# Plain fp32 matmuls in the w_o and S5 projections, DMAs taken off GpSimd's queue, and a larger weight pool, in a two-block fp32 model on one core

## The chip, the core and the metric

The kernel runs on one core of a Trainium2 chip, as one launch. The engines are TensorE (PE: matmul and transposes; its weight loads show as PEld), VectorE (DVE), ScalarE (ACT), GpSimd (POOL) and SyncE (SP), which here only issues DMAs. Each runs its own instructions in order and waits on semaphores. The metric is device time in microseconds from start to end of one execution; smaller is better.

## The reference

The input x has 256 tokens of 1024 features, all in fp32. The first block is attention and a mixture of experts, the second an S5 mixer, a gated FFN with a causal convolution (ffn0), a forgetting attention (fox) and another FFN (ffn1), and a last norm.

```python
h = rms_norm(x, ln1_g); z = h @ w_in                       # first block
o_a = window_gqa(q_a, k_a, v_a, rel_bias, a_sink)          # 8 heads of 64, window 128
o_b = latent_attention(c_q, c_kv, k_rope, ...)             # 8 heads, 64 + 32 rotated
x = x + concat([rms_norm(o_a), rms_norm(o_b)]) @ w_o       # 1024 x 1024
x = x + expert_choice_ffn(rms_norm(x), w_router, w_gate, w_up, w_down)   # 16 experts of 1024 x 1024 x 3
# second block; shift, scale, gate = silu(c) @ ada_w + b, four times
u = h @ w_in; hs = scan(lb, u @ bb); y = gelu(hs @ c + d * u)            # S5, complex diagonal state
m = (y * sigmoid(y @ w_glu)) @ w_out
h = h + gate * m;  h = h + gate * conv_ffn(...)            # 1024 -> 2 x 2816 -> 1024
F = cumsum(log_sigmoid(h @ w_f + b_f)); s = q.k / 8 + F[t] - F[s]        # fox, causal, 16 heads
h = h + gate * (softmax(s) @ v @ w_out);  h = h + gate * conv_ffn(...)
```

## The kernel before

The stages run one after the other: attention, experts, S5, ffn0, fox, ffn1, final norm. Activations sit on the 128 partitions, either by token (two halves of 128) or by feature (8 x 128).

**Matmuls.** Most large projections use `mm3` (line 367): both operands are split into a rounded part and a rest (`hi`, `lo`, type fp32r), and three matmuls are added up, hi x hi, hi x lo and lo x hi. `mm` (line 360) issues one matmul; on plain fp32 operands it shows as two records in the trace. The experts' gate and up projections and the attention scores are already plain. A `Pair` holds hi and lo; `split` (line 397) makes one from a result in PSUM, hi by ACT and lo by DVE.

**Weights.** `plan` (line 225) lists loads in the order in which they are to be issued. `fill` (line 259) issues them on SP's queue, each into a slot of 8 KB per partition (1 MB in all), as long as slots are free:

```python
while self.pos < min(n, len(self.loads)) and self.used + self.room + max(0, self.hires - self.his) < NSLOT and self.wused < self.cap:
```

`prep` (line 271) splits a weight that has landed: `whi` on ACT (for w_oa and w_ob on POOL, line 287) and `wlo` on DVE or on POOL (line 291), into two further slots, and the raw one is freed. `done` gives slots back when the last matmul has been issued, and calls `fill` again. NSLOT is 22. `MIDS` (9) is the number of 2 KB tiles that `m2k` hands out in turn (`z`, `rot`, `g`, `sq` and others). `weights(room, look, hires)` sets per stage how many slots are kept back. Room for both and for GpSimd's DMA ring comes from the same memory.

**Attention** (`attn_block`). Scores, softmax and weighting run by head pairs; `finish` (line 960) scales an output and splits it into `o`; `w_o` (line 1024) multiplies by w_oa or w_ob, 4 x 4 x 2 matmuls of 512 columns, each as three. `bqk`, `p`, `mx` and `bkT` are tiles of the latent heads' queries and keys, the softmax and the transposed keys. While this runs, `fill` fetches the first experts' w_gate and w_up.

**S5** (`s5`, line 1465). `u(n)` (n = 0 to 3) is a projection of 256 features, followed by a transpose into `V` on DVE. `states(n)` multiplies by a table `S`, copies PSUM to `z` on ACT, transposes to `re` and `im`, turns them by cos and sin on DVE and POOL (tiles `rot`), scans along the chunk on DVE, and turns back. `outputs(n)` makes `y`, gelu on ACT, transposes it on DVE (`yt`) and splits it (`yh`, `yl`). `glu(n)` multiplies by w_glu, 64 matmuls of 256 columns in all, each as three. The order written in the code is u0, u1, states 0, u2, states 1, outputs 0, u3, states 2, outputs 1, states 3, outputs 2 and 3, then glu and the output projection (`acc`); a scheduler orders each engine's instructions from it.

**Fox** (`fox`, line 1740). The forget gate's cumulated logs `F` are written to DRAM (`f_dram`) and read back as `nF`, broadcast over partitions, both on POOL's queue. `project_v` and `project` use twelve slices of fox_w_in. Rows of gates go through DRAM as well (`row_dram`, lines 661 and 668, SP's queue); ada_t is the weight of the shifts, scales and gates.

Of the kernel before, what the change touches and what calls it, by code (L numbers as in the profile page):

```python
# [24 lines left out]
NSLOT = 22  # L25
MIDS = 9
# [128 lines left out]
class Kern:  # L155
# [115 lines left out]
    def prep(self, upto, must=True):  # L271

        while self.prepos < min(upto, self.pos):
# [8 lines left out]
            elif split:  # L282
# [6 lines left out]
                for n in range(0, shape[1], k):  # L289
                    f = slice(n, n + k)  # L290
                    for ins in (hc(hi[:, f], t[:, f]), e.tensor_tensor(lo[:, f], t[:, f], hi[:, f].bitcast(F32), op=OP.subtract)):  # L291
                        if self.pin:
                            self.tc.keep_in_program_order(ins)
                        self.behind(ins)
                        if key == ("s5_w_in", 0) and n >= KN.get("pw", 2) * k:
                            self.behind(ins, self.pows)
# [140 lines left out]
    def norm_T(self, l, b, perm=False, before=None, pump=0):  # L437
# [7 lines left out]
        x = self.pair("xT", [128, 8, T])  # L445
        self.touch(x.hi[:, 0], x.lo[:, 0])
# [7 lines left out]
    def norm_T_(self, x, t, ab, perm, before, hv):  # L454
# [12 lines left out]
        for q in range(2):  # L467
# [4 lines left out]
            for c in range(0, 4, m):  # L472
# [3 lines left out]
                hi, lo = (y[:, 4 * q + c:4 * q + c + m, t * 128:(t + 1) * 128] for y in (x.hi, x.lo))  # L476
                if perm:
                    b = b.rearrange("p d (k s) -> p d s k", s=4)
                    hi, lo = (y.rearrange("p d (s k) -> p d s k", s=4) for y in (hi, lo))
                end = self.split(Pair(hi, lo), b)  # L480
# [195 lines left out]
    def attn_plan(self, ada):  # L676
# [17 lines left out]
        for x in KN.get("ord", "A" * (8 - KN.get("am", 3)) + "oooo" + "A" * KN.get("am", 3)):  # L694
# [4 lines left out]
            else:  # L699
                name = ("w_oa", "w_ob")[no // 2]  # L700
                self.plan((name, no % 2), i[name][no % 2], (128, 4, 512), self.nc.gpsimd)
# [28 lines left out]
    def attn_block(self):  # L730
# [163 lines left out]
        o = self.pair("o", [128, 8, T])  # L894
# [65 lines left out]
        def finish(kind, n, p, mx):  # L960
# [8 lines left out]
            e = Pair(*(x.rearrange("p (t q) -> p t q", t=2) for x in (o[:, u].hi, o[:, u].lo)))  # L969
            self.split(e, po, self.c("out_" + kind, n))  # L970
# [53 lines left out]
        def w_o(s, t, n):  # L1024
            w = self.get(("w_oa" if s == 0 else "w_ob", n))
            acc = self.ps("wo")
            for j in range(4):
                self.mm3(acc, o[:, 4 * s + j, t * 128:(t + 1) * 128], w[:, j], j == 0, j == 3)
# [49 lines left out]
        self.free(2)  # L1078
# [169 lines left out]
    def s5_plan(self, early):  # L1248
# [6 lines left out]
        for n in range(4):  # L1255
            if n == KN.get("s5e", 1):
                self.loads += end
            self.plan(("s5_w_in", n), i["s5_w_in"][n], (128, 8, 256), self.pool("s5", n))

        def rest():  # L1260
            for n in range(4):
                self.plan(("s5_w_glu", n), i["s5_w_glu"][n], (128, 8, 256))
# [32 lines left out]
    def s5_params(self):  # L1295
# [5 lines left out]
        gp.dma_start(Wa[:, 0:4], i["s5_cols"])  # L1301
        bc = self.slot("bc", [128, 4, 32, 16])
        gp.dma_start(bc, i["s5_bc"])
# [161 lines left out]
    def s5(self, before):  # L1465
        nc = self.nc
        v, gp = nc.vector, nc.gpsimd
        xT = self.norm_T(0, 0, perm=True, before=before)
# [60 lines left out]
        def outputs(n):  # L1529
# [40 lines left out]
        self.free(2)  # L1570
# [9 lines left out]
        def glu(n):  # L1580
# [26 lines left out]
        self.free(2)  # L1607
# [132 lines left out]
    def fox(self, before):  # L1740
# [268 lines left out]
```

## Time and profile before

| | us |
|---|---|
| median of 3 runs | 1329.26 (1327.92 to 1331.11) |
| profiled execution, its own time | 1327.95 |
| its span | 1326.2 |
| PE busy | 1109.0 (84%) |
| DVE busy | 706.3 (53%) |
| ACT busy | 422.3 (32%) |
| POOL busy | 151.4 (11%) |

The span leaves 1.75 us of the execution's own time outside. Busy counts instructions that run; one that overlaps another of its engine counts once. DMA moved 379 MB, 286 GB/s on average. The granted clock is the share of its full speed that TensorE was given; its mean was 0.895. The stages' places in the span: attention to about 150 us, routing to 175, the experts to 625, S5 to 765, fox from about 965 to 1110, with an FFN behind each of the two.

### The profile page before, as it was taken

The page shows a single profiled execution, that of the slowest core. Times are in us where ns is not written, and L with a number is a line of the kernel's source. Part 1 is how long each engine was busy: PE and PEld are TensorE (multiplying, and loading weights), DVE is VectorE, ACT ScalarE, POOL GpSimd, SP SyncE. Part 2 cuts the span into 40 slices and gives each one's busy share as a digit, 9 for nine tenths or more (in the row PEclk, how much of TensorE's full clock was granted, in tenths as well). Part 3 has the DMA queues.
Part 4 walks back from the last instruction along what each step waited for, and adds up shares of the span by engine and source line. Part 5 has one row for each costly group of instructions (what it writes and reads, how often), then busy time and mean ns, then how long its engine had stood idle before and what let it go on. Part 6 is the DMA issues. An engine that isn't in the chain of part 4 may idle for free.

```text
span 1326.2 us, 19901 instructions
## 1 busy us (share of the span) xinstructions
PE 1109.0 (84%) x7935; PEld 761.5 (57%) x7935; DVE 706.3 (53%) x1570; ACT 422.3 (32%) x879; POOL 151.4 (11%) x153
## 2 busy tenths in 40 slices
PE   8958898666676866575978999999999978999997
PEld 7646631101121411011757879998879756999986
DVE  6696410117159507003677667755557755577662
ACT  7244110000000100002233455643444543656541
POOL 2472000010000000000133300000010023300001
PEclk9979998767877877766988999999999989999999
DMA  8945989999999999998586455549655747247330
GB/s 329 409 146 221 351 344 419 420 419 420 420 419 420 419 420 419 420 418 361 190 317 224 152 215 222 192 162 358 224 226 191 299 178 269 100 156 272 145 125 32
DMA packets 61385, 379.38 MB, mean 286 GB/s; under 512 B 6723, under 2 KB 8499, under 8 KB 19692
## 3 DMA queue, kind: packets, MB, share of 16 engines
q1 hardware_dynamic: 60364, 374.49, 71.2%
q0 software_dynamic: 496, 3.23, 0.6%
q8 instruction: 62, 1.02, 0.3%
q10 hardware_dynamic: 432, 0.40, 0.1%
q14 instruction: 31, 0.25, 0.1%
HBM read 376.96 MB, written 1.13 MB: 285 GB/s over the span
## 4 chain that ended last, share of the span: by engine, by line
PE 52%; DMA 29%; DVE 8%; issue 2%; ACT 2%; POOL 1%; SPq 0%; POOLq 0%; DVEq 0%; ACTq 0%
PE up L361 19%; DMA w<-in_w_down_dram 12%; PE acc L361 12%; DMA w<-in_w_up_dram 9%; DMA w<-in_w_gate_dram 6%; PE qk L361 2%; PE v L361 2%; PE wo L361 2%; PE pg L361 1%; PE u L361 1%; PE xe L361 1%; PE glu L361 1%; PE pu L361 1%; PE sc L361 1%; DMA row<-row_dram 1%
## 5 line engine op out<-in xcount | busy, mean ns | idle before, releaser
L291 DVE TENSOR_TENSOR wlo<-w,whi 128x512 fp32r<-128x512 f32 (+3 forms) x316 | 236.0, 804 | 60.3 <-ACT whi L291 53.1
L291 ACT CAST whi<-w 128x512 fp32r<-128x512 f32 (+3 forms) x336 | 209.2, 698 | 74.7 <-PE acc L361 25.8
L361 PE MATMUL up<-xTh,whi 128*128 128x256 f32 x704 | 200.2, 285 | 1.1 <-ACT whi L291 0.9
L361 PE MATMUL up<-xTl,whi 128*128 128x256 f32 x704 | 199.6, 284 | 0.2 <-DVE xTl L402 0.2
L361 PE MATMUL up<-xTh,wlo 128*128 128x256 f32 x704 | 199.1, 284 | 0.0
L361 PEld LDWEIGHTS up<-xTh,whi 128*128 128x128 f32 x704 | 135.2, 192 | 5.1 <-ACT cv L1693 1.7
L361 PEld LDWEIGHTS up<-xTl,whi 128*128 128x128 f32 x704 | 135.3, 192 | 0.7 <-DVE xTl L402 0.7
L361 PEld LDWEIGHTS up<-xTh,wlo 128*128 128x128 f32 x704 | 135.0, 192 | 0.2 <-DVE wlo L291 0.2
L361 PE MATMUL py<-w,aT 128*32 128x512 f32 x512 | 93.5, 823 | 49.6 <-DMA w<-in_w_down_dram 49.6
L361 PE MATMUL pg<-w,xe 128*32 128x512 f32 x512 | 86.0, 749 | 34.0 <-DMA w<-in_w_gate_dram 34.0
L361 PE MATMUL pu<-w,xe 128*32 128x512 f32 x512 | 84.4, 735 | 35.6 <-DMA w<-in_w_up_dram 35.6
L361 PEld LDWEIGHTS py<-w,aT 128*32 128x32 f32 x512 | 12.3, 124 | 117.8 <-DMA w<-in_w_down_dram 100.5
L361 PE MATMUL acc<-whi,gTh 128*128 128x512 f32 (+1 forms) x220 | 76.5, 348 | 0.0
L361 PE MATMUL acc<-whi,gTl 128*128 128x512 f32 (+1 forms) x220 | 76.4, 347 | 0.0
L361 PE MATMUL acc<-wlo,gTh 128*128 128x512 f32 (+1 forms) x220 | 76.2, 347 | 0.0
L404 DVE SCALAR_TENSOR_TENSOR yl<-py,gcol,yh 128x512 fp32r<-128x512 f32 x8 | 6.0, 751 | 120.1 <-ACT yh L403 120.1
L361 PEld LDWEIGHTS pu<-w,xe 128*32 128x32 f32 x512 | 13.5, 119 | 95.1 <-DMA w<-in_w_up_dram 78.8
L291 POOL TENSOR_TENSOR wlo<-w,whi 128x512 fp32r<-128x512 f32 x36 | 48.7, 1385 | 139.5 <-ACT whi L291 92.5
L361 PEld LDWEIGHTS pg<-w,xe 128*32 128x32 f32 x512 | 12.5, 118 | 87.7 <-DMA w<-in_w_gate_dram 75.0
L1219 DVE TENSOR_TENSOR a<-pu,a 128x512 f32<-128x512 f32 x8 | 5.5, 692 | 107.5 <-PE pu L361 107.5
L403 ACT ACTIVATE yh<-py,gcol 128x512 fp32r<-128x512 f32 x8 | 5.5, 687 | 144.7 <-PE py L361 144.7
L1646 POOL TENSOR_TENSOR h<-h,gm 128x512 f32<-128x512 f32 x8 | 10.4, 1294 | 346.2 <-DVE gm L1645 346.1
(465 smaller groups left out, 2166.3 us busy)
## 6 DMA issues: line engine op xcount, KB each, us to landing
w<-in_w_gate_dram SPq DMA_DIRECT2D x64, 1024.0 KB, 19.3
w<-in_w_up_dram SPq DMA_DIRECT2D x64, 1024.0 KB, 19.9
w<-in_w_down_dram SPq DMA_DIRECT2D x64, 1024.0 KB, 19.9
w<-in_ada_t_dram SPq DMA_DIRECT2D x48, 1024.0 KB, 8.2
w<-in_ffn_w_up_dram SPq DMA_DIRECT2D x44, 1024.0 KB, 5.0
w<-in_ffn_w_down_dram SPq DMA_DIRECT2D x22, 1024.0 KB, 6.6
w<-in_fox_w_in_dram SPq DMA_DIRECT2D x12, 1024.0 KB, 5.7
row<-row_dram SPq DMA_DIRECT2D x24, 256.0 KB, 8.6
```

The costliest lines, as they stand in the source:

```text
L291: for ins in (hc(hi[:, f], t[:, f]), e.tensor_tensor(lo[:, f], t[:, f], hi[:, f].bitcast(F32), op=OP.subtract)):
L361: r = self.nc.tensor.matmul(out, lhsT, rhs, start=start, stop=stop)
L403: return (nc.scalar.mul(dst.hi, src, a), nc.vector.scalar_tensor_tensor(dst.lo, src, a, dst.hi.bitcast(F32), op0=OP.mult, op1=OP.subtract))
L404: nc.vector.scalar_tensor_tensor(dst.lo, src, a, dst.hi.bitcast(F32), op0=OP.mult, op1=OP.subtract))
L1219: nc.vector.tensor_tensor(a, pu, a, op=OP.mult)
L1646: ins.append((nc.gpsimd if a < KN.get("pa", 512) else nc.vector).tensor_tensor(self.h[:, t, a:e], self.h[:, t, a:e], tm, op=OP.add))
```

## The change

Plain fp32 for w_o, for u and for glu: `mm` in place of `mm3`, no split of these weights and of `o`, `xT` (in S5) and `y`, each of which takes one slot where it took two. The DMAs of f_dram go to ACT's queue and those of nF, s5_cols and s5_bc to SP's; GpSimd's DMA ring is set to 1 KB. NSLOT goes from 22 to 23 and MIDS from 9 to 12. In S5, states 0 stands ahead of u1 (`s5o`), and the slots kept back ahead of it go from 8 to 9 (`w_body0`).

```diff
-NSLOT = 22
-MIDS = 9
+NSLOT = 23
+MIDS = 12
...
-"s5o": 0, ... "w_body0": [8, 0, 3],
+"s5o": 1, ... "w_body0": [9, 0, 3],
...
-                self.plan((name, no % 2), i[name][no % 2], (128, 4, 512), self.nc.gpsimd)
+                self.plan((name, no % 2), i[name][no % 2], (128, 4, 512), False)
...
-        o = self.pair("o", [128, 8, T])
+        o = self.slot("o", [128, 8, T])
...
-            e = Pair(*(x.rearrange("p (t q) -> p t q", t=2) for x in (o[:, u].hi, o[:, u].lo)))
-            self.split(e, po, self.c("out_" + kind, n))
+            s_.mul(o[:, u].rearrange("p (t q) -> p t q", t=2), po, self.c("out_" + kind, n))
...
-                self.mm3(acc, o[:, 4 * s + j, t * 128:(t + 1) * 128], w[:, j], j == 0, j == 3)
+                self.mm(acc, o[:, 4 * s + j, t * 128:(t + 1) * 128], w[:, j], j == 0, j == 3)
...
-            self.plan(("s5_w_in", n), i["s5_w_in"][n], (128, 8, 256), self.pool("s5", n))
+            self.plan(("s5_w_in", n), i["s5_w_in"][n], (128, 8, 256), False)
...
-                self.plan(("s5_w_glu", n), i["s5_w_glu"][n], (128, 8, 256))
+                self.plan(("s5_w_glu", n), i["s5_w_glu"][n], (128, 8, 256), False)
...
-        gp.dma_start(Wa[:, 0:4], i["s5_cols"])
+        nc.sync.dma_start(Wa[:, 0:4], i["s5_cols"])
         bc = self.slot("bc", [128, 4, 32, 16])
-        gp.dma_start(bc, i["s5_bc"])
+        nc.sync.dma_start(bc, i["s5_bc"])
...
-        xT = self.norm_T(0, 0, perm=True, before=before)
+        xT = self.norm_T(0, 0, perm=True, before=before, whole=True)
...
-                    self.mm3(b[:, t * 256:(t + 1) * 256], xT[:, k, t * 128:(t + 1) * 128], w[:, k], k == 0, k == 7)
+                    self.mm(b[:, t * 256:(t + 1) * 256], xT[:, k, t * 128:(t + 1) * 128], w[:, k], k == 0, k == 7)
...
-                ys.append(self.pair("y", [128, 8, T]))
-            y = ys[0][:, 2 * n:2 * n + 2]
-            yy = self.m2k("yt", [128, 2, T])
-            v.transpose(yy.rearrange("p g t -> p (g t)"), g)
-            nc.scalar.copy(y.hi, yy)
-            v.tensor_tensor(y.lo, yy, y.hi.bitcast(F32), op=OP.subtract)
+                ys.append(self.slot("y", [128, 8, T]))
+            v.transpose(ys[0][:, 2 * n:2 * n + 2].rearrange("p g t -> p (g t)"), g)
...
-                        self.mm3(bs[f], w[:, k, f * 128:(f + 1) * 128], yp[:, k], k == 0, k == 7)
+                        self.mm(bs[f], w[:, k, f * 128:(f + 1) * 128], yp[:, k], k == 0, k == 7)
...
-            y = self.m2k("yf", [128, 2, T])
-            gp.tensor_tensor(y, yp[:, 2 * n:2 * n + 2].hi.bitcast(F32), yp[:, 2 * n:2 * n + 2].lo.bitcast(F32), op=OP.add)
+            y = yp[:, 2 * n:2 * n + 2]
...
-        nc.gpsimd.dma_start(self.f_dram, nF_)
+        nc.scalar.dma_start(self.f_dram, nF_)
...
-            nc.gpsimd.dma_start(nF[n], self.f_dram[8 * n:8 * n + 8].partition_broadcast(128))
+            nc.sync.dma_start(nF[n], self.f_dram[8 * n:8 * n + 8].partition_broadcast(128))
...
-    nc = _bacc.Bacc("TRN2", target_bir_lowering=False, num_devices=1)
+    nc = _bacc.Bacc("TRN2", target_bir_lowering=False, num_devices=1, dynamic_dma_scratch_size=1024)
```

How the instructions stand, first on POOL in the second half of attention (`whi` and `wlo` are the parts of w_oa and w_ob, `bqk` the latent queries and keys, `sq` squares of the outputs). Before:

```order
L990 TENSOR_TENSOR bqk_519<-bqk_519,early_87 128x8x32 x2
L287 TENSOR_TENSOR whi_749<-w_584,ones_88 128x512 x4
L291 TENSOR_TENSOR wlo_750<-w_584,whi_749 128x512 x4
L287 TENSOR_TENSOR whi_862<-w_609,ones_88 128x512 x4
L291 TENSOR_TENSOR wlo_863<-w_609,whi_862 128x512
L287 TENSOR_TENSOR whi_926<-w_735,ones_88 128x512 x4
L291 TENSOR_TENSOR wlo_863<-w_609,whi_862 128x512 x3
L976 TENSOR_TENSOR sq_854<-sq_854,sq_917 128x256
L291 TENSOR_TENSOR wlo_927<-w_735,whi_926 128x512 x4
L976 TENSOR_TENSOR sq_854<-sq_854,sq_976 128x256
```

And now:

```order
L865 TENSOR_TENSOR bqk_519<-ro_566 128x8x16
L866 TENSOR_TENSOR bqk_519<-ro_566 128x8x16
L993 TENSOR_TENSOR bqk_519<-bqk_519,early_87 128x8x32 x2
L979 TENSOR_TENSOR sq_836<-sq_836,sq_888 128x256
L979 TENSOR_TENSOR sq_836<-sq_836,sq_936 128x256
L979 TENSOR_TENSOR sq_836<-sq_836,sq_977 128x256
L381 TENSOR_TENSOR early_87<-early_87,small_86 128x2
```

The eight groups on w_o's weights are gone (the first stand further up), and what is left of POOL's work there stands close together.

On PE at the start of S5's states (`u` the projections, `ada` a side matmul for later shifts, `z` the copy of S's result). Before, all 96 matmuls of u0 and u1 stand ahead of these rows:

```order
L361 MATMUL S_3808<-S_2153,V_3659 32x256 x8
L361 MATMUL ada_3742<-w_3796,sc_329 32x512 x4
L375 MATMUL re_3806<-small_86,z_3817 128x4x32
L375 MATMUL im_3807<-small_86,z_3817 128x4x32
L375 MATMUL re_3806<-small_86,z_3817 128x4x32
L375 MATMUL im_3807<-small_86,z_3817 128x4x32
L361 MATMUL S_3823<-S_2153,V_3659 32x256 x8
L361 MATMUL u_3879<-whi_3722,xTh_3599 128x256
L361 MATMUL u_3879<-wlo_3723,xTh_3599 128x256
L361 MATMUL u_3879<-whi_3722,xTl_3600 128x256
```

And now, where 16 matmuls of u0 stand ahead:

```order
L359 MATMUL S_3554<-S_2040,V_3532 32x256 x8
L359 MATMUL ada_3625<-w_3649,sc_329 32x512 x4
L373 MATMUL re_3552<-small_86,z_3563 128x4x32
L373 MATMUL im_3553<-small_86,z_3563 128x4x32
L373 MATMUL re_3552<-small_86,z_3563 128x4x32
L373 MATMUL im_3553<-small_86,z_3563 128x4x32
L359 MATMUL S_3569<-S_2040,V_3532 32x256 x8
L359 MATMUL u_3632<-w_3452,xT_3478 128x256 x11
L373 MATMUL re_3552<-small_86,z_3578 128x4x32
L373 MATMUL im_3553<-small_86,z_3578 128x4x32
L373 MATMUL re_3552<-small_86,z_3578 128x4x32
L373 MATMUL im_3553<-small_86,z_3578 128x4x32
```

u1's matmuls have moved behind the first states' S, and eleven of them stand between S and the transposes `re` and `im`.

On DVE, about the first state step (`V` the transposed projection, `rot` the tiles of the step). Before, the transposes of u0 and u1 precede it:

```order
L1485 STREAM_TRANSPOSE V_3659<-u_3660 128x256 x2
L291 TENSOR_TENSOR wlo_3733<-w_3595,whi_3732 128x512 x4
L1485 STREAM_TRANSPOSE V_3711<-u_3747 128x256 x2
L1504 TENSOR_TENSOR rot_3838<-re_3806,tcos_3149 128x512
L1505 TENSOR_TENSOR rot_3839<-im_3807,tsin_3150 128x512
L1507 TENSOR_TENSOR rot_3840<-im_3807,tcos_3149 128x512
L1508 TENSOR_TENSOR rot_3841<-re_3806,tsin_3150 128x512
L1519 MEMSET rot_3864 128x8
```

And now only that of u0 does, and those of u1 and u2 stand behind the step's last four rows:

```order
L1522 TENSOR_TENSOR rot_3610<-rot_3584,tcos_3036 128x8x63
L1525 TENSOR_TENSOR rot_3611<-rot_3584,tsin_3037 128x8x63
L1523 TENSOR_TENSOR rot_3612<-rot_3586,tsin_3037 128x8x63
L1526 TENSOR_TENSOR rot_3613<-rot_3586,tcos_3036 128x8x63
L1487 STREAM_TRANSPOSE V_3622<-u_3632 128x256 x2
L1487 STREAM_TRANSPOSE V_3659<-u_3660 128x256 x2
L1506 TENSOR_TENSOR rot_3713<-re_3681,tcos_3036 128x512
L1507 TENSOR_TENSOR rot_3714<-im_3682,tsin_3037 128x512
```

On SP's queue in fox, about the write to row_dram (its read stands further down). Before:

```order
L267 DMA w_7452<-in_fox_w_in_dram 128x2048
L267 DMA w_7513<-in_ada_t_dram 128x2048
L267 DMA w_7553<-in_fox_w_in_dram 128x2048
L267 DMA w_7604<-in_ada_t_dram 128x2048
L267 DMA w_7655<-in_fox_w_in_dram 128x2048
L267 DMA w_7706<-in_ada_t_dram 128x2x1024
L267 DMA w_7768<-in_fox_w_in_dram 128x2048
L661 DMA row_dram_78<-gr_7834 16x128
L267 DMA w_7951<-in_fox_w_in_dram 128x2048
L267 DMA w_8012<-in_ada_t_dram 128x2x1024
L267 DMA w_8033<-in_fox_w_in_dram 128x2048
```

And now:

```order
L267 DMA w_6679<-in_fox_w_in_dram 128x2048
L267 DMA w_6681<-in_fox_w_in_dram 128x2048
L1795 DMA nF_6906<-f_dram 128x2048
L1795 DMA nF_6907<-f_dram 128x2048
L267 DMA w_6978<-in_ada_t_dram 128x2048
L267 DMA w_7039<-in_fox_w_in_dram 128x2048
L267 DMA w_7079<-in_ada_t_dram 128x2048
L267 DMA w_7130<-in_fox_w_in_dram 128x2048
L267 DMA w_7181<-in_ada_t_dram 128x2x1024
L267 DMA w_7232<-in_fox_w_in_dram 128x2048
L267 DMA w_7294<-in_fox_w_in_dram 128x2048
L267 DMA w_7477<-in_ada_t_dram 128x2x1024
```

The two reads of nF stand in this queue now, with ada_t and fox_w_in behind them, and eleven of the twelve fox_w_in loads precede the write to row_dram, where ten did (the last two rows here lie just ahead of it).

## Rows read from the trace of the kernel before

**Rows 1.** Page, chain that ended last: shares of the span by line.

```profile
PE up L361 19%; DMA w<-in_w_down_dram 12%; PE acc L361 12%; DMA w<-in_w_up_dram 9%; DMA w<-in_w_gate_dram 6%; PE qk L361 2%; PE v L361 2%; PE wo L361 2%; PE pg L361 1%; PE u L361 1%; PE xe L361 1%; PE glu L361 1%; PE pu L361 1%; PE sc L361 1%; DMA row<-row_dram 1%
```

**Rows 2.** Stretches: us, busy us of PE, PEld, DVE, ACT, POOL, granted clock, DMA share, GB/s.

```profile
170.00:180.00 10.00, 10.00 (x45) 3.03 (x44) 1.50 (x2) 1.37 (x2) 0.00 (x0) 0.94 0.62 241
...
500.00:600.00 100.00, 64.55 (x368) 11.36 (x363) 28.84 (x118) 4.50 (x10) 0.00 (x0) 0.74 1.01 419
...
620.00:640.00 20.00, 14.86 (x92) 11.89 (x89) 15.48 (x28) 10.65 (x22) 1.52 (x2) 0.70 0.32 124
```

**Rows 3.** Timeline of SP's queue, prefetch of expert weights: start, us, operation.

```profile
173.01 0.33 SPq L267 DMA_DIRECT2D w<-in_w_gate_dram  x1
```

**Rows 4.** Timeline of DVE, attention: start, us, line, operation.

```profile
60.39 4.96 DVE L981 TENSOR_SCALAR early<-early 128x16 f32<-128x16 f32 x1
...
80.28 4.49 DVE L951 TENSOR_SCALAR p<-p,mx 128x256 f32<-128x256 f32 x4
...
108.50 1.14 DVE L951 TENSOR_SCALAR p<-p,mx 128x256 f32<-128x256 f32 x4
```

**Rows 5.** Timeline of POOL, the same stretch.

```profile
59.50 4.99 POOL L291 TENSOR_TENSOR wlo<-w,whi 128x512 fp32r<-128x512 f32 x4
```

**Rows 6.** Waits of PE, 60 to 115 us: us in total, times, longest us.

```profile
PE bqT L375 <- DVE bqk L989: 8.7, 1, 8.7
PE pTp L375 <- DVE p L951: 3.8, 2, 2.5
PE sc L361 <- DVE bkT L358: 2.8, 1, 2.8
```

**Rows 7.** Chain in order of time, attention and S5: start, us, what, count of records.

```profile
105.32 1.74 PE sc L361 x8
...
132.39 5.67 PE wo L361 x24
...
633.09 11.47 PE u L361 x94
...
732.17 8.35 PE glu L361 x68
```

**Rows 8.** Timeline of DVE, S5: first and last of four state steps.

```profile
651.55 0.69 DVE L1504 TENSOR_TENSOR rot<-re,tcos 128x512 f32<-128x512 f32 x1 [6.18 <-PE re L375]
...
700.38 0.69 DVE L1504 TENSOR_TENSOR rot<-re,tcos 128x512 f32<-128x512 f32 x1 [1.58 <-PE re L375]
```

**Rows 9.** Chain in order of time, S5.

```profile
631.65 0.43 PE u L361 x2
...
658.84 0.68 DVE rot L1523
659.62 0.59 ACT z L1497
...
715.78 0.72 DVE yt L1550
...
718.47 0.88 PE glu L361 x5
...
725.86 5.75 PE glu L361 x28
...
740.53 4.56 PE acc L361 x20
```

**Rows 10.** Chain in order of time, fox.

```profile
968.25 8.33 DMA w<-in_ada_t_dram
...
1014.00 0.99 PE ada L361 x8
...
1033.79 5.68 DMA w<-in_fox_w_in_dram
```

**Rows 11.** Timeline of POOL, fox.

```profile
994.85 0.58 POOL L1795 DMA_DIRECT2D f_dram<-F  x1 [20.64 <-DVE F L1794]
```

**Rows 12.** Timeline of SP's queue, fox.

```profile
987.81 0.33 SPq L267 DMA_DIRECT2D w<-in_ada_t_dram  x1
```

More of the change, by code (lines that the diff above doesn't have):

```diff
@@ L294, in prep @@
                         self.behind(ins)
-                        if key == ("s5_w_in", 0) and n >= KN.get("pw", 2) * k:
-                            self.behind(ins, self.pows)
                 self.state[key] = [t, Pair(hi, lo)]
@@ L435, in fetch, with norm_T @@
             self.rows_of[l, b] = self.row_in(self.need("ada", l, b), 4)
-    def norm_T(self, l, b, perm=False, before=None, pump=0):
+    def norm_T(self, l, b, perm=False, before=None, pump=0, whole=False):
         ab = self.rows_of.pop((l, b), None) or self.row_in(self.need("ada", l, b), 4)
@@ L444, in norm_T @@
             self.last(self.end)
-        x = self.pair("xT", [128, 8, T])
-        self.touch(x.hi[:, 0], x.lo[:, 0])
+        if whole:
+            x = self.slot("xT", [128, 8, T])
+            self.touch(x[:, 0])
+        else:
+            x = self.pair("xT", [128, 8, T])
+            self.touch(x.hi[:, 0], x.lo[:, 0])
         for t in range(2):
@@ L475, in norm_T_ @@
                     self.tr(b[:, d], hn[q][:, (c + d) * 128:(c + d + 1) * 128])
-                hi, lo = (y[:, 4 * q + c:4 * q + c + m, t * 128:(t + 1) * 128] for y in (x.hi, x.lo))
+                ys = [y[:, 4 * q + c:4 * q + c + m, t * 128:(t + 1) * 128]
+                      for y in ((x.hi, x.lo) if isinstance(x, Pair) else (x,))]
                 if perm:
                     b = b.rearrange("p d (k s) -> p d s k", s=4)
-                    hi, lo = (y.rearrange("p d (s k) -> p d s k", s=4) for y in (hi, lo))
-                end = self.split(Pair(hi, lo), b)
+                    ys = [y.rearrange("p d (s k) -> p d s k", s=4) for y in ys]
+                end = self.split(Pair(*ys), b) if len(ys) == 2 else ((v.tensor_copy if q else nc.scalar.copy)(ys[0], b),)
             if t >= 2 - KN.get("bar", 1):
@@ L1077, in attn_block @@
             self.logits(1)
-        self.free(2)
+        self.free()
     def moe_plan(self):
@@ L1476, in u @@
             V = Vs[n] = self.m2k("V", [128, 2, 8, 32])
-            self.pin = n == 0
             w = self.get(("s5_w_in", n))
@@ L1569, in s5 @@
         self.pump(KN.get("s5p2",9))
-        self.free(2)
+        self.free()
         states(2)
@@ L1606, in s5 @@
                 self.fetch(0, 1)
-        self.free(2)
+        self.free()
         self.weights(*kw("w_s50", 1, 2, 6))
```

2 rows, old and new, of the table KN are left out of this document.

## The prediction

> **What bounds the kernel now.** I read the page first, then the stretches, then each stage's waits. The chain that ended last lies on TensorE (PE) and on the expert weights' DMA by turns [rows 1]. That share mixes two regimes, and the stretches separate them [rows 2]. From about 180 to 620 us, in the experts, the DMA engines are busy all the time (share 1.01 at 419 GB/s) and no compute instruction sets the end. A load of 1024 KB costs 2.5 us there (1.049 MB / 419 GB/s). Ahead of that stretch the DMA still had room: its share is 0.62 between 170 and 180 us, because the queue waits for a weight slot; it gets one at 173.01, when the first expert's work has begun [rows 3]. So the experts end at "when the queue starts to run full" plus bytes over rate, and what comes earlier in attention and routing comes out 1:1 at 620 us, as does every megabyte that has landed before.
>
> Attention itself waits on VectorE (DVE) while GpSimd (POOL) works beside it. One DVE operation on 16 columns took 4.96 us [rows 4]; it lies beside four POOL subtractions of 4.99 us [rows 5]. The same four `p` scalings took 4.49 us at 80.28, with POOL busy, and 1.14 us at 108.50, with POOL nearly idle [rows 4]. PE waits for those results: 8.7 us for `bqk`, 3.8 for `p` and 2.8 for `bkT` between 60 and 115 us, 15.3 in all [rows 6].
>
> In S5 the chain runs through the DVE's four state steps. The first starts at 651.55 and the fourth at 700.38 [rows 8], so one each 16.3 us. Right behind the rotation at 658.84 comes the copy `z` of the next step at 659.62 [rows 9]: it has waited for that rotation, whose tile it takes over (there are 9 tiles of 2 KB).
>
> **The change, part by part.** *Price of a matmul.* The `sc` matmuls are already plain fp32: 8 records of 256 columns take 1.74 us, 0.2175 each [rows 7]; one matmul is two records, so 0.435. Three split ones take 3 x 0.122 = 0.366 (`u`: 11.47 us / 94) or 0.369 (`glu`: 8.35 / 68) [rows 7]. For 512 columns, two records are 0.87 by doubling `sc`, and three split ones 0.71 (`wo`: 5.67 / 24). The added PE time: `wo` 32 x 0.15 = +4.8 us (its own records); `u` 64 x 0.069 = +4.4; `glu` 64 x 0.066 = +4.2.
>
> *Attention.* Four `whi` and four `wlo` groups leave POOL. What comes back: 4.8 at the 16-column operation, if it shrinks to the 0.2 us that its width suggests; 3.35 at the scalings (4.49 - 1.14); and for the four bqk operations and the small maxima from 71 to 103 us, whose undisturbed price the trace lacks, 4.5 by estimate, since the wait for `bqk` is 8.7. That is 12.7 us, between 8.2 (the first two) and 15.3 (all the waits of [rows 6]). The `wo` stage ran PE back to back and pays +4.8 in full. **Net -8, bounds -3.4 to -10.5.**
>
> *23rd slot and smaller tiles in use.* One megabyte more lands before the DMA runs full: **-2.5**. The idle share between 170 and 180 us (0.38 x 10 = 3.8 us) has room for it; bounds 0 and -5, since a plain weight holds one slot where a split one held two.
>
> *S5.* The first state step: nT ends at 631.65, then 16 `u` (7.0), 1.5 for the granted clock (0.70 in this stretch [rows 2]), the ada matmuls 1.9, the V transposes 0.8, S, z and re 2.1, S again 1.0, eleven `u` 4.8, re 0.5: 651, read as 650.5 with some overlap. Before it was 651.55. So half the projections and the higher price cancel. A step holds the DVE for about 9.1 us (651.55 to the fourth rotation behind 658.84). The order puts the transposes of `u1` and `u2` behind step 0: 659.6 + 1.5. From z to the next step before (659.62 to about 667.9) took 8.3 us, of which 3.4 were `u` matmuls that stand elsewhere now: 4.9. Second step at 666.0. For the third, V is there and 12 tiles let z run beside the second step. Its floor is 9.1 + 1.4 for two transposes = 10.5; `u3`'s 7.0 us still stands on PE in that gap, so I take 14.4: 680.4. For the fourth 11.1: 691.5, which is -8.9 against 700.38. Beside the last step PE now does 24 `glu` matmuls (10.4 us, where before 52 records took 6.4), of which I let 1.3 reach the last `y`: -7.6 at the transpose behind it, before at 715.78 [rows 9]. From there to the acc matmuls at 740.53 it was 24.75 us, 6.5 of them a stop of `glu` from 719.35 to 725.86 [rows 9]. Now it is 0.7 for the transpose, no `yh` and `yl`, 40 remaining `glu` matmuls at 0.435 = 17.4, and a stop of 0 to 6.5, of which I take 4.4 (ACT's table load, the sigmoids and the splits of y2 stay): 22.5, so -2.2. The other `u` matmuls at the lower clock: +1.5. **Net -8.3, taken as -8; bounds -3** (the period falls only by the `u` moved) **and -12** (10.5 for the third step too).
>
> *Fox.* Before, PE waited 8.33 us for an ada load and later the chain ran through 5.68 us for a fox_w_in weight issued at 1033.79 [rows 10], behind the write to row_dram. One more slot brings the first 2.5 us forward; one more fox_w_in is issued ahead of that write. Against it: the reads of nF now stand in SyncE's (SP's) queue and wait for f_dram's write, with ada_t and fox_w_in behind them. The write was issued at 994.85 [rows 11] and landed some 4.5 later, so an ada load that left at 987.81 [rows 12] can leave 11 us late. With the 8.33 us of [rows 10] it lands at about 1007.5 and is used at 1014.00 [rows 10]: hidden by 6 us. If that cover goes, +4. **Net -3, bounds +4 and -8.** The other stages (both FFNs) are PE-bound and untouched: 0. The s5_cols and s5_bc loads move to SP among the first experts' loads: their bytes move anyhow, 0.
>
> *Sum:* -8 - 2.5 - 8 - 3 = -21.5 us, from the profiled run's own 1327.95 us to 1306.45. The median of the runs is 1.3 us above that run, hence **1308 us**.
>
> **The rivals.** *A, slower.* The POOL and DVE work was cover, and PE's added 4.8 + 4.4 + 4.2 = 13.4 us are all on the path: 1329.3 + 13.4 = 1343. This decides if PE's waits of [rows 6] keep their length and the state steps stay 16.3 apart. For it: `wo` and `glu` run back to back on the path. Against: `u` stands beside DVE steps, and two operations show four times their price beside POOL. The Trainium skill (FP8 and Floating Point Precision, TensorE Precision Notes) counts four passes for true fp32; at 0.24 and 0.122 per pass one pass more would make 32 x 0.24 + 128 x 0.122 = 23 us and 1352. The trace disagrees in the size: four passes take 0.435, or 0.109 each [rows 7].
>
> *B, one of the two large terms fails* (S5 keeps its period, since z and re wait on PE's order: 0 to +2 there; or attention's gain isn't seen behind the experts, because the weights prefetched don't land earlier): -21.5 + 8 to +10, so about 1318. For it: u3 does stand between the steps.
>
> *C, SP stalls in fox:* +4 in place of -3: 1315.
>
> *D, more:* attention -10.5, slot -5 and S5 -12, with fox at -3: 1329.3 - 30.5 = 1299. For it, the waits of [rows 6] sum to 15.3 and two-slot weights become one-slot ones.
>
> *E, a held DVE operation loses one POOL instruction only:* 4.99 / 4 = 1.25 us at the 16-column one instead of 4.8. Attention then gives 3.5 less: 1311. Against it stands the 4.96 us itself, as long as all four [rows 4, 5]. The Trainium skill (SBUF — State Buffer, Who interferes with whom) says so: whoever issues first holds the shared port pair for that whole instruction and the other blocks until its end, and a DVE operation with one SBUF input outside the two-port modes isn't held at all. By that rule 1311; the trace agrees that something holds it and shows more than one instruction.
>
> **How the numbers follow.** The forecast, 1303 to 1313, has 0.45; B 0.22; C 0.10; D 0.10; E 0.05; A 0.08. The bounds of the single terms added give -2.4 and -35.5, or 1327 and 1294; not all fall at one end, so for 8 in 10 I take 1294 to 1322, which leaves out A and the worst of B and C together. A measurement of this kernel can tell about 0.2%, 2.7 us. Slower: A and a little of B with C together, 0.09; within 0.2%: where two of the terms fail, 0.05; faster: 0.86.
>
> **What would show it.** In the profile after: no `whi` or `wlo` on POOL between 50 and 105 us, the 16-column operation under 1 us, PE's wait for `bqk` under 3 us, and routing 8 us earlier; `wo` records at 0.43. The DMA share reaches 1.0 some 8 us earlier, and S5's normalised tile stands at about 621. State steps at intervals near 15.5, 14.4 and 11.1, and the acc matmuls about 101 us after it, where it was 109 (740.53 - 631.65). In fox, the nF reads on SP at about 4.5 us behind the write, with no PE wait on ada. I am wrong if PE's waits in attention only change their name, if the DMA runs full no earlier than 175 us, or if the state steps stay at 16 us.

## The result, and the profile after

The changed kernel takes 1309.28 us (median of 4 runs, 1305.73 to 1311.31) against 1328.59 for the kernel before beside it: the ratio is 0.9854, 95% interval 0.9822 to 0.9885. That is -19.3 us, where 1308 us, -21, was forecast. In a later set of runs it was 1306.81 against 1326.89 (0.9843, 0.9826 to 0.9860). The total hides that one term came out larger than its bound and another with the other sign. The profiled execution took 1308.50 us, its span is 1306.4.

The page of the changed kernel, busy time and the chain that ended last by line (answers to [rows 1]):

```profile
PE 1105.4 (85%) x7775; PEld 751.2 (58%) x7775; DVE 661.9 (51%) x1523; ACT 401.5 (31%) x841; POOL 102.4 (8%) x112
...
PE 57%; DMA 30%; DVE 7%; ACT 2%; issue 2%; POOL 1%; SPq 0%; POOLq 0%; DVEq 0%; ACTq 0%
PE up L359 20%; DMA w<-in_w_down_dram 12%; DMA w<-in_w_up_dram 11%; PE acc L359 10%; DMA w<-in_w_gate_dram 6%; PE qk L359 3%; PE wo L359 2%; PE u L359 2%; DMA row<-row_dram 2%; PE v L359 2%; PE ada L359 2%; PE glu L359 2%; PE zl L359 1%; PE zq L359 1%; PE xe L359 1%
```

POOL fell from 151.4 to 102.4 us and DVE from 706.3 to 661.9; PE is busy for nearly as long as before (1105.4, 1109.0 before), although it has fewer instructions.

Where the time went, by landmarks in the two traces (start of the first operation of a kind):

| landmark | before | after | gained in this stretch |
|---|---|---|---|
| first `wo` matmul | 115.09 | 99.48 | 15.6 |
| last `wo` matmul ends (chain) | 151.85 | 141.72 | -5.5 |
| first expert slot freed (SP) | 173.01 | 162.09 | 0.8 |
| first `u` of S5 | 631.30 | 616.50 | 3.9 |
| first `acc` of S5 | 740.36 | 713.45 | 12.1 |
| first `up` of ffn0 | 769.32 | 743.26 | -0.9 |
| first `v` of fox | 978.03 | 952.40 | -0.4 |
| first `acc` of fox | 1087.90 | 1067.67 | -5.4 |
| first `up` of ffn1 | 1127.51 | 1108.10 | -0.8 |
| end of span | 1326.2 | 1306.4 | 0.4 |

**Attention.** DVE's timeline in the changed kernel (start, us, line, operation; line 984 is line 981 of before):

```profile
60.85 0.17 DVE L984 TENSOR_SCALAR early<-early 128x16 f32<-128x16 f32 x1
...
67.38 0.68 DVE L992 TENSOR_TENSOR bqk<-bqk,early 128x512 f32<-128x512 f32 x1
67.98 0.68 DVE L994 TENSOR_TENSOR bqk<-bqk,early 128x512 f32<-128x512 f32 x1
```

And PE's waits there (us in total, times, longest):

```profile
PE bqT L373 <- DVE bqk L992: 3.0, 1, 3.0
...
PE pTp L373 <- DVE p L955: 0.7, 1, 0.7
```

In the kernel before, the operations on bqk lay beside POOL's work on w_o's weights:

```profile
71.75 1.52 DVE L989 TENSOR_TENSOR bqk<-bqk,early 128x512 f32<-128x512 f32 x1
```

```profile
71.64 5.42 POOL L287 TENSOR_TENSOR whi<-w,ones 128x512 fp32r<-128x512 f32 x4
```

The 16-column operation takes 0.17 us where it took 4.96 [rows 4]. The operations on bqk take 0.68, where they took 1.52 beside POOL, and PE waits 3.0 us for them, where it waited 8.7 [rows 6]. The wait for `bkT` is gone.

**`wo`, then the load queue.** The chain in order of time, and the DMA's stretch (us, busy us of PE, PEld, DVE, ACT, POOL, granted clock, DMA share, GB/s; answers to [rows 2, 7]):

```profile
118.76 7.06 PE wo L359 x16
...
127.34 3.56 PE wo L359 x8
```

```profile
162.09 0.33 SPq L267 DMA_DIRECT2D w<-in_w_up_dram  x1
```

```profile
160.00:170.00 10.00, 10.00 (x47) 3.19 (x45) 1.50 (x2) 1.38 (x2) 0.00 (x0) 1.00 0.56 210
170.00:180.00 10.00, 10.00 (x58) 3.90 (x58) 1.50 (x2) 1.42 (x3) 0.00 (x0) 1.00 0.98 383
```

Sixteen records take 7.06 us and eight 3.56, so 0.44 each, 0.88 for a matmul, and the DMA runs full from about 170 us instead of 180.

**S5.** The four state steps on DVE, and the chain behind the last `y` (answers to [rows 8, 9]):

```profile
635.24 0.69 DVE L1506 TENSOR_TENSOR rot<-re,tcos 128x512 f32<-128x512 f32 x1 [9.65 <-PE re L373]
...
650.48 0.69 DVE L1506 TENSOR_TENSOR rot<-re,tcos 128x512 f32<-128x512 f32 x1 [4.79 <-PE re L373]
...
664.37 0.69 DVE L1506 TENSOR_TENSOR rot<-re,tcos 128x512 f32<-128x512 f32 x1 [3.44 <-PE re L373]
...
675.81 0.69 DVE L1506 TENSOR_TENSOR rot<-re,tcos 128x512 f32<-128x512 f32 x1 [1.62 <-PE re L373]
```

```profile
692.68 0.72 DVE y L1550
693.45 2.01 PE glu L359 x8
...
699.98 13.81 PE glu L359 x64
713.79 20.56 PE acc L359 x107
```

The steps come 15.2, 13.9 and 11.4 us apart, where they came every 16.3. `glu` stops from 695.46 to 699.98, 4.5 us, where it stopped 6.5.

**Fox.** The chain in the changed kernel, about the last kT copy, and DVE in the kernel before at the same place:

```profile
1045.66 7.33 PE qk L359 x47
1053.01 1.23 DVE wlo L291
1054.24 4.98 DVE p L1822 x4
1059.22 0.61 DVE kT L1764
...
1059.87 1.71 PE sc L359 x7
```

```profile
1076.91 1.01 DVE L1825 TENSOR_SCALAR p<-p,mx 128x128 f32<-128x128 f32 x4
1077.83 2.35 DVE L291 TENSOR_TENSOR wlo<-w,whi 128x1024 fp32r<-128x1024 f32 x2
1080.10 0.68 DVE L1767 COPY kT<-qk 128x512 f32<-128x512 f32 x1
```

```profile
1053.71 5.36 POOL L291 TENSOR_TENSOR wlo<-w,whi 128x512 fp32r<-128x512 f32 x4 [104.15 <-ACT whi L291]
```

Here the changed kernel loses. Before, the scaling of `p` (1.01 us) stood ahead of the subtraction `wlo` on DVE. Now half of that `wlo` stands ahead of it; it gets its slot only when the last `qk` matmuls are through at 1053.0, so the scaling starts at 1054.2, beside POOL's `wlo` of 5.36 us, and takes 4.98 us. The copy `kT` and the next scores wait for it. The 47 `qk` records ahead of it took 7.33 us at a granted clock of 0.79 (1045 to 1053 us); before, as many took 5.85.

### The profile page after: what moved, and what is told of

Read it like the earlier page. It is cut to its first block, busy times and chain, and to the rows that moved or that the text cites. A ratio compares the mean times of both kernels' runs of the same rounds, so it can differ in the third digit from the quotient of the medians.

```text
span 1306.4 us, 19378 instructions
## 1 busy us (share of the span) xinstructions
PE 1105.4 (85%) x7775; PEld 751.2 (58%) x7775; DVE 661.9 (51%) x1523; ACT 401.5 (31%) x841; POOL 102.4 (8%) x112
## 4 chain that ended last, share of the span: by engine, by line
PE 57%; DMA 30%; DVE 7%; ACT 2%; issue 2%; POOL 1%; SPq 0%; POOLq 0%; DVEq 0%; ACTq 0%
PE up L359 20%; DMA w<-in_w_down_dram 12%; DMA w<-in_w_up_dram 11%; PE acc L359 10%; DMA w<-in_w_gate_dram 6%; PE qk L359 3%; PE wo L359 2%; PE u L359 2%; DMA row<-row_dram 2%; PE v L359 2%; PE ada L359 2%; PE glu L359 2%; PE zl L359 1%; PE zq L359 1%; PE xe L359 1%
## 5 line engine op out<-in xcount | busy, mean ns | idle before, releaser
L291 DVE TENSOR_TENSOR wlo<-w,whi 128x512 fp32r<-128x512 f32 (+4 forms) x284 | 214.1, 815 | 51.7 <-ACT whi L291 44.2
L291 ACT CAST whi<-w 128x512 fp32r<-128x512 f32 (+4 forms) x304 | 191.6, 706 | 59.6 <-PE acc L359 23.8
L359 PE MATMUL pg<-w,xe 128*32 128x512 f32 x512 | 89.4, 777 | 35.3 <-DMA w<-in_w_gate_dram 35.2
L359 PE MATMUL py<-w,aT 128*32 128x512 f32 x512 | 81.8, 744 | 40.6 <-DMA w<-in_w_down_dram 40.5
L1691 DVE SCALAR_TENSOR_TENSOR cv<-up,small,cv 128x255 f32<-128x255 f32 x44 | 20.9, 482 | 53.8 <-ACT cv L1690 53.6
L1221 ACT ACTIVATE a<-pg 128x512 f32<-128x512 f32 x8 | 4.8, 597 | 134.0 <-PE pg L359 134.0
```

The source lines that it names most:

```text
L359: r = self.nc.tensor.matmul(out, lhsT, rhs, start=start, stop=stop)
L1221: nc.scalar.activation(a, pg, AF.Silu)
L1691: v.scalar_tensor_tensor(cv[:, 1:], a[:, :T - 1], cw[1], cv[:, 1:], op0=OP.mult, op1=OP.add)
```

## The experiments

The theory after the result: (1) attention gains because POOL's work on w_o's weights had held DVE; (2) the experts pass it on and the 23rd slot adds to it; (3) S5 gains by the tiles and the order, hardly by the plain matmuls themselves; (4) fox loses by an order on DVE that nobody asked for, and not by SP's wait. Rivals stand with each run. "Stage" below is the time between landmarks of the table. Executions of one kernel spread by 3 to 10 us, so what is read of a mechanism is read from the stage in the profile, and the time beside it.

**w_o alone, on the kernel before.** 22 slots, 9 tiles, all else as before:

```diff
-                self.plan((name, no % 2), i[name][no % 2], (128, 4, 512), self.nc.gpsimd)
+                self.plan((name, no % 2), i[name][no % 2], (128, 4, 512), False)
...
-        o = self.pair("o", [128, 8, T])
+        o = self.slot("o", [128, 8, T])
...
-                self.mm3(acc, o[:, 4 * s + j, t * 128:(t + 1) * 128], w[:, j], j == 0, j == 3)
+                self.mm(acc, o[:, 4 * s + j, t * 128:(t + 1) * 128], w[:, j], j == 0, j == 3)
```

> The kernel before with the w_o projection alone made plain (22 slots, 9 tiles of 2 KB, S5 split, DMAs of GpSimd as before). Theory (POOL's work on w_o's weights held DVE): the 16-column operation falls from 4.96 to about 0.2 us, PE's wait for bqk from 8.7 to 3, the first freed expert slot comes at about 162 instead of 173.0, S5's first u at about 621 instead of 631.65, and that gain of 11 us stands at the end of S5 too: 1318, or 1323 if the order of DVE in fox loses its 5.7 us here as well. Rival (most of attention's gain came with the 23rd slot and the larger tile pool): the first freed slot at 170 or later, 1326 to 1329. Second rival (the experts don't pass it on): slot at 162 but u at 630, 1328.

1320.25 us, ratio 0.9938 (0.9918 to 0.9957), 6.9 us less than before. The 16-column operation takes 0.17 us, the wait for bqk is 3.1, the first `wo` starts at 97.89 (before 115.09) and the first freed slot comes at 158.33. First `u` is at 616.12, so the experts pass it on. The profiled execution was the fastest of nine (1312.85), and some 3 us of its lead over the profile before lie in the routing, where the first 8 `xe` records took 3.70 us instead of 6.67. Fox (first `v` to first `acc`) is 113.0 us, before 109.9: the scaling of `p` has the same 5.08 us as in the changed kernel, with 22 slots and GpSimd's DMAs in place. So both rivals fall, and the order that costs in fox needs neither the slot nor the queues. S5, whose code here is that of before, took 105.2 us (721.27 - 616.12) instead of 109.1: by some 4 us it moves without an edit of its own.

**w_o still split, but off POOL.**

```diff
-                if key[0] in ("w_oa", "w_ob", "w_qb", "w_kvb") and KN.get("hip", 1):
+                if key[0] in ("w_qb", "w_kvb") and KN.get("hip", 1):
...
-                self.plan((name, no % 2), i[name][no % 2], (128, 4, 512), self.nc.gpsimd)
+                self.plan((name, no % 2), i[name][no % 2], (128, 4, 512), True)
```

> The kernel before with w_o still split into three matmuls, but its weights rounded on ACT and subtracted on DVE instead of both on POOL. It takes away POOL's work beside attention and nothing else, and adds 16 x 0.6 us to ACT and to DVE. Theory (it is POOL beside DVE that costs): the 16-column operation under 0.6 us, PE's wait for bqk under 4, the first freed slot near 163 to 168, since three matmuls at 0.24 are even cheaper than a plain one at 0.43 but DVE has 10 us more to do; 1318 to 1325. Rival (what returned was the split work as such, whoever does it): no gain or a loss, slot at 173 or later, 1329 to 1336.

1322.97 us, ratio 0.9968 (0.9948 to 0.9987): faster by 4.1 us, although DVE and ACT took over all of the work. Its DVE timeline and PE's wait:

```profile
61.57 0.16 DVE L981 TENSOR_SCALAR early<-early 128x16 f32<-128x16 f32 x1
...
68.19 0.68 DVE L989 TENSOR_TENSOR bqk<-bqk,early 128x512 f32<-128x512 f32 x1
```

```profile
PE bqT L375 <- DVE bqk L989: 1.6, 1, 1.6
```

The same operations shrink, to 0.16 and 0.68 us, with three matmuls per product left in place; first `wo` is at 107.61, the freed slot at 165.91. That is theory 1: it is POOL beside DVE that cost, and of the 15.6 us at the first `wo` 7.5 come back by moving the work alone. The rest would be work that doesn't exist any more in the changed kernel (DVE's 16 `wlo` take 11.5 us here); that isn't tested apart. In fox this run, too, has half of the `wlo` ahead of the scaling, with 22 slots and GpSimd's DMAs, and the stage takes 115.4 us:

```profile
1071.34 1.22 DVE L291 TENSOR_TENSOR wlo<-w,whi 128x1024 fp32r<-128x1024 f32 x1 [0.52 <-PE qk L361]
1072.49 5.08 DVE L1825 TENSOR_SCALAR p<-p,mx 128x128 f32<-128x128 f32 x4
```

**S5's two projections alone, on the kernel before** (9 tiles, 22 slots, states 0 behind u1; the edits are those of `u`, `outputs` and `glu` in the diff ahead).

> The kernel before with S5's u and glu alone made plain (w_o split, 22 slots, 9 tiles, states 0 behind u1 as before). Theory of the prediction (the tiles and the order let z run beside the step, plain matmuls by themselves only take yh, yl and the splits away): state steps still about 15 to 16 us apart, the stretch from the first u to acc 104 to 107 instead of 108.9 (it is 97.1 in the changed kernel); 1324 to 1327. Rival (the plain matmuls alone give it, since the splits no longer stand on DVE and ACT): steps 12 to 14 us apart and 97 to 99 us, 1317.

1326.76 us, ratio 1.000 (0.9983 to 1.0017): nothing. First `u` to first `acc` is 108.4 us (738.80 - 630.38; before 109.1), even less gain than expected; state steps 16.8, 13.4 and 15.7 us apart. Plain matmuls by themselves are not what S5 gained. Fox, with w_o as before, takes 110.4 us, and the scaling of `p` there stands ahead of the whole `wlo`, at 1.01 us.

**The changed kernel with 9 tiles** (`MIDS = 12` to `MIDS = 9`).

> The changed kernel with 9 tiles of 2 KB instead of 12. Theory (with plain matmuls alone S5 gains nothing, as the run with S5 alone showed; the tiles let z of the next step run beside the present one): z waits for the rotation's tile again, state steps 15 to 17 us apart instead of 15.2, 13.9 and 11.4, first u to acc 102 to 108 instead of 97: 1314 to 1320. Rival (it is the order with states 0 ahead of u1): S5 stays at 97 to 99, 1309 to 1311.

1312.97 us, ratio 0.9890 (0.9863 to 0.9916). S5 takes 103.1 us instead of 97.0 and the steps are 15.3, 13.9 and 15.9 apart; only the last one lost, 4.5 us. ACT's waits name the tile:

```profile
ACT z L1499 <- DVE rot L1525: 3.5, 1, 3.5
```

That is half of the theory: leaving out the three tiles costs 6.1 us, but the steps 15.3 and 13.9 are set by something else. It is PE: the rows of the changed kernel name its `re` as what ended DVE's 4.79 and 3.44 us of idle time ahead of those steps.

**The changed kernel with u1 ahead of states 0 again** (`"s5o": 1` to `"s5o": 0`).

> The changed kernel with u1 ahead of states 0 again. Theory (tiles do most of it, order gives the first step an earlier start): the first state step some 6 us later after the first u than the present 18.7, as in the run with S5 alone (25.7), the later ones 11 to 14 apart, first u to acc 99 to 103: 1311 to 1315. Rival (the order is the whole gain): 106 to 109, 1318 or more. Second rival (the order does nothing, since u1 has to be done anyway): 97, 1309.

1312.31 us, ratio 0.9890 (0.9851 to 0.9930). The first step starts 26.5 us behind the first `u` (643.53 - 617.02), where it was 18.7; the others are 10.7, 12.8 and 13.1 apart, and S5 takes 100.4 us. So leaving out the order costs 3.4 us and leaving out the tiles 6.1. Of the 12.1 some 2.6 are left for the plain matmuls and all else; no run has the tiles and the order with split matmuls, so that share isn't shown.

**The changed kernel with 22 slots** (`NSLOT = 23` to `NSLOT = 22`).

> The changed kernel with 22 weight slots instead of 23, all else kept. Theory of the prediction (one megabyte less has landed when the DMA runs full): the experts end 2.5 us later after the first freed slot (464.2 to 457 us now: 616.5 less 162.1 is 454.4; then 457), 1312; with the 4.1 us that this stretch really gained, up to 1313. Rival (the freed halves of the split weights fill the DMA anyway, as the run with w_o alone had its first u at 616.1 with 22 slots): 1309.

1310.79 us, ratio 0.9880 (0.9857 to 0.9903), which the time alone can't tell from 23 slots. The stage can: from the first freed slot (162.57) to the first `u` (619.77) it is 457.2 us, with 23 slots 454.4, before 458.3. One slot is worth 2.8 us in the experts, as 1 MB over the rate says (2.5).

**The changed kernel with f_dram and nF on GpSimd's queue again.**

```diff
-        nc.scalar.dma_start(self.f_dram, nF_)
+        nc.gpsimd.dma_start(self.f_dram, nF_)
...
-            nc.sync.dma_start(nF[n], self.f_dram[8 * n:8 * n + 8].partition_broadcast(128))
+            nc.gpsimd.dma_start(nF[n], self.f_dram[8 * n:8 * n + 8].partition_broadcast(128))
```

> The changed kernel with the write of f_dram and the two reads of nF on GpSimd's queue again, the ring staying at 1 KB. Theory (SP's wait behind the write is hidden, fox lost its time elsewhere): loads of ada_t and fox_w_in leave up to 7 us earlier, the fox stage (first v to first acc) stays at 115, within 1 us; 1308 to 1310. Rival (SP's wait is what fox lost): the stage falls to 110, 1304.

1306.10 us, ratio 0.9855 (0.9824 to 0.9885), the same ratio as the changed kernel's. Fox is 113.8 us instead of 115.3, a little more than expected. That isn't the queue's doing: the last `qk` matmuls ran at a granted clock of 1.00 (1043 to 1049 us) and not 0.79, in 5.84 us instead of 7.33, and the run with 9 tiles, whose nF is on SP, takes 113.8 in fox as well.

```profile
1043.22 5.84 PE qk L359 x47
```

The queue does move. SP in the changed kernel and here:

```profile
970.46 0.80 SPq L1795 DMA_DIRECT2D nF<-f_dram  x2
971.35 0.38 SPq L267 DMA_DIRECT2D w<-in_ada_t_dram  x1
```

```profile
955.88 0.33 SPq L267 DMA_DIRECT2D w<-in_ada_t_dram  x1
958.72 0.33 SPq L267 DMA_DIRECT2D w<-in_fox_w_in_dram  x1
```

The next ada load leaves 971.35 - 952.40 = 19.0 us behind the first `v`, and here 5.9, where up to 7 us earlier was expected. These 13 us are hidden; the scaling of `p` still takes 5.08 us here.

**DVE's order in fox mended, on the changed kernel.** One dependence puts the subtraction for the fourth fox_w_out weight behind the scaling of `p` for the sixth pair of heads:

```diff
+                        if key == ("fox_w_out", 3):
+                            self.behind(ins, self.p5)
...
-                    v.tensor_scalar(ps_[t][:, j], ps_[t][:, j], mx[:, 4 + k:5 + k], None, op0=OP.mult)
+                    e = v.tensor_scalar(ps_[t][:, j], ps_[t][:, j], mx[:, 4 + k:5 + k], None, op0=OP.mult)
+            if i == 5:
+                self.last(e, after=self.p5)
```

> The changed kernel with one more dependence: the subtraction for the fourth fox_w_out weight stands on DVE behind the scaling of p of the sixth head pair, where the kernel before had it. Theory (fox lost 5.7 us because half of that subtraction, which waits for a slot until the last qk is through, stood ahead of the scaling, which then ran beside POOL's wlo at 4.98 instead of 1.0 us): the scaling at about 1 us, the fox acc matmuls start 4 to 6 us earlier, 1303 to 1305. Rival (the loss comes from POOL's wlo or the lower clock there, and stays): 1308 to 1310, with the wait moved to the next DVE operation.

1304.07 us, ratio 0.9833 (0.9792 to 0.9873). DVE at that place:

```profile
1050.64 1.01 DVE L1825 TENSOR_SCALAR p<-p,mx 128x128 f32<-128x128 f32 x4
1052.74 0.69 DVE L1767 COPY kT<-qk 128x512 f32<-128x512 f32 x1 [1.09 <-PE qk L362]
1053.35 4.54 DVE L292 TENSOR_TENSOR wlo<-w,whi 128x1024 fp32r<-128x1024 f32 x2
```

The scaling takes 1.01 us again, three us earlier, and fox is 110.1 us (1062.08 - 952.02), before 109.9. Mending the order takes back the whole loss; POOL's `wlo` is still there and now lies beside a `wlo` of DVE.

**On one chip: the changed kernel again, and two variants of the mended one.** The second has nF on GpSimd's queue too, the third has no POOL work on weights in fox ahead of the first `acc`:

```diff
-        return self.nc.gpsimd if n < KN.get("pool_" + name, 0) else True
+        return self.nc.gpsimd if (0 if name != "ffn1" else 1) <= n < KN.get("pool_" + name, 0) else True
```

> The changed kernel as it is, on the same chip as the two variants that follow, so that differences of a few us are read on one chip. 1306 to 1311; the fox stage (first v to first acc) 115 us, S5 (first u to acc) 97, the first freed expert slot between 158 and 163, as the runs of the same order so far differ there by the granted clock alone.

> The run with DVE's order in fox mended, and in addition f_dram and nF on GpSimd's queue again. If the order alone is what fox lost, the stage is at 110 as in that run and the time 1302 to 1305, 4 to 6 below the changed kernel on this chip; if SP's wait costs too, the stage falls to 107 to 109 and the time to 1300 to 1302.

> The run with DVE's order in fox mended, and in addition the first ffn1 weight's subtraction on DVE instead of POOL, so that POOL does nothing on weights in fox ahead of the first acc. Theory (with the scaling of p out of the way, POOL's wlo holds nothing that the end waits for): fox stays at 110 or loses 1 to 2 us, since DVE has 2.5 us more to do: 1303 to 1307. Rival (POOL beside DVE still costs there): 107 to 108, 1301.

1306.81, 1304.20 and 1301.03 us; ratios 0.9843 (0.9826 to 0.9860), 0.9823 (0.9793 to 0.9852) and 0.9814 (0.9791 to 0.9837). Fox is 115.3, 110.1 and 109.1 us. So mending the order is worth 5.2 us in the stage, and nF's queue nothing on top. In the time the second is 2.6 us below the changed kernel, where 4 to 6 were expected, and the intervals overlap: the gain is shown in the stage alone. The 0.9 us of the third are not POOL's: they lie ahead of the copy `kT`, in the `qk` matmuls, which ran at a granted clock of 0.79 in the second (1047 to 1055 us) and of 1.00 in the third (1041 to 1049). DVE about `kT`, in the second and in the third:

```profile
1055.09 0.69 DVE L1767 COPY kT<-qk 128x512 f32<-128x512 f32 x1 [1.08 <-PE qk L362]
```

```profile
1048.94 0.69 DVE L1767 COPY kT<-qk 128x512 f32<-128x512 f32 x1
```

From there to the first `acc` it is 9.4 and 9.6 us, so POOL's last `wlo` costs nothing that this shows. The third is the fastest kernel tried, 5.8 us below the changed one on the same chip by the medians, with intervals that overlap a little; 4.7 us of the lead of its profiled execution were there ahead of fox, in stages that are the same in both.

## Why the prediction was right, and where it was not

The forecast was -21.5 us in four terms; the traces show -10.9 (10.1 of them by the end of `wo`), -3.9, -12.1 and +5.4, and small losses of 1.7 elsewhere. It was right in direction and mechanism for three terms, and near in total because errors cancelled: against the forecast fox came out 8.4 us worse and the rest 1.7, attention 2.9 better, the experts 1.4 and S5 4.1. That the sum came so close is luck.

**Price of a matmul: right.** 0.87 by doubling `sc` was 0.88 in the `wo` records. (Less 0.71 that is 0.16 and not 0.15, so 5.1 us for `wo` by its own rows.) Rival A, in which this price is all that is seen, fell: the `wo` stage grew by 5.5 us (forecast 4.8) and everything around it shrank by more.

**Attention: mechanism right, size too small.** -12.7 ahead of `wo` was forecast and -15.6 came, a little over what all the waits of [rows 6] allowed (15.3). The term that was mis-sized is the one with no undisturbed row: four operations on bqk, at 0.68 instead of 1.52, give 3.4 by themselves, and the small maxima and the second half the rest; 4.5 was allowed for them together. Net -10.1 at the end of `wo` (bound -10.5). The run off POOL shows the cause.

**E, a held operation loses one POOL instruction only,** was wrong in its place and right elsewhere. The 16-column operation lost 4.8 us as a single instruction. It ended at 65.35, when POOL's unbroken run of subtractions [rows 5] and two short operations behind them was over, at 65.32:

```profile
64.84 0.48 POOL L862 TENSOR_TENSOR bqk<-ro 128x128 f32<-128x128 f32 x1
```

In fox four scalings lost 4.0 us in all, and each took about as long as one POOL instruction: 4.98 / 4 = 1.25 against 5.36 / 4 = 1.34 for one POOL instruction. The Trainium skill (SBUF — State Buffer, Who interferes with whom) has the second case, a lock held for one instruction. The first doesn't fit it; that POOL's next instruction won the lock again each time would explain it, and no run tests that.

**The 23rd slot: right.** -2.5 was forecast; 2.8 by the run with 22 slots, 3.9 in the trace. Rival B's doubt, that the experts might not pass attention's gain on, fell: the first `u` came earlier by the freed slot's 10.9 and 3.9 more.

**S5: steps right, sum too cautious.** The first step was put 18.9 us behind the first `u` and came 18.7 behind, in part by luck: the 1.5 us for a lower clock did not come, and the ada matmuls ahead of it took 3.7 us instead of 1.9. The intervals 15.5, 14.4 and 11.1 were 15.2, 13.9 and 11.4; the stop of `glu` 4.4 was 4.5. One reason failed: 12 tiles were to help the third step, by letting z run beside the second, but with 9 tiles it comes 13.9 us behind the second too. The tiles act at the fourth.

Yet the stage gained 12 and not 8. The last step started 9.8 us earlier relative to the first `u` where 8.9 was said. The 1.3 us that the moved `glu` matmuls were to cost the last `y` came, as 1.5 (it follows the last step by 16.9 us, 15.4 before). Two terms were mis-sized. Behind the last `y` 22.5 us were forecast and 20.8 measured (713.45 - 692.68), since 36 `glu` matmuls were left there and not 40: 72 records in 2.01 + 13.81 us. And the 1.5 for the lower clock of the other `u` matmuls was nothing: 42 of their records ran in 9.07 us, 0.216 each, the price at full clock. The clock went the other way. It was granted at 1.00 from 616.5 to 716.5 us, where in the 100 us behind the first `u` before it was between 0.83 and 0.98 (five stretches of 20 us). One group of `S` matmuls on the chain, before and after:

```profile
661.37 1.87 PE S L361 x16
```

```profile
647.65 1.00 PE S L359 x16
```

So part of the 12 us is the clock, and no run separates it from the rest.

**Fox: the step that failed.** "Net -3" became +5.4, outside its bound of +4. Two things went wrong. First, the gain was read from the wrong quantity. The 8.33 us of [rows 10] are the time of an ada load from issue to landing, as a link of the chain, and not a wait of PE, which worked through most of them. Its wait for that load was 0.9 us:

```profile
PE ada L361 <- DMA w<-in_ada_t_dram: 0.9, 1, 0.9
```

Nor did PE wait for the fox_w_in load of 5.68 us; between the first `v` and the first `acc` its only wait for a load was 1.6 us. Both waits are gone in the changed kernel and nothing came of it: the first `v` comes 209.1 us behind the first `up` of ffn0, 208.7 before, with PE busy for 207.1 of them, 205.3 before. Second, the danger was looked for on SP's queue; it was on DVE's, and the forecast had only read SP's queue and the operations that the diff names in fox. In the two kernels with w_o changed alone or moved off POOL, whose diffs don't touch fox, the same half of a `wlo` stands ahead of the scaling; in the one with S5 changed alone it doesn't. So an edit of w_o, far upstream, goes with DVE's order in fox. Rival C had the sign and the place, by a wrong cause.

In these traces the order's price has two parts: the scaling waits for a `wlo` that waits for a slot (2.0 us of idle time ahead of it in the changed kernel, 0.5 with w_o alone), and it then lies beside POOL (4.98 instead of 1.01). No run has the one without the other. Mended, the scaling ended at 1051.65 and POOL began at 1053.32.

## What to carry to other kernels

Work put on GpSimd because it is idle can cost what DVE does beside it: price it by the same DVE operation with and without it, both of which one trace often has. A cheaper operation pays where its buffers and its order let it: here plain matmuls alone gave nothing in S5, and without the tiles or the order 6 or 3 of the 12 us were lost. A link of the chain that is a load gives its time in flight; what it can give back is what the engine waited for it, and that stands in the waits. And where a scheduler places instructions, compare every engine's order in every stage, also those the diff doesn't touch; one dependence won back 5 us in its stage.

## What the runs showed of the hardware

Beside POOL's back-to-back instructions a DVE operation with a single input (128 x 16) took 4.96 us instead of 0.17, and ended 0.03 us behind the last of them; operations with two inputs (128 x 512) took 1.52 instead of 0.68 us. The first 8 `xe` records of the routing took 5.14 us in one execution of the changed kernel and 5.29 in another, and 3.70 in three of its variants with the same attention; between 150 and 160 us the granted clock was 0.73 where they took 5.14, and 1.00 in two of the three with 3.70. That chance alone moves everything behind it by up to 1.6 us, and 6.67 was seen in the kernel before. The 47 `qk` records of fox took 5.84 or 7.33 us in the same way.
